# Hybrid decoder step: the S5 tables dealt between preparation and loop, U loaded earlier, gate tiles dealt anew

## The chip, the cores and the metric

One core of a Trainium2 chip runs the kernel. The engines are TensorE (PE, and PEld for its weight loads), VectorE (DVE), ScalarE (ACT), GpSimd (POOL) and SyncE (SP), which here only issues DMAs. The metric is the device time of one execution in microseconds (us), lower is better, given as the median of the runs.

## The reference

One inference step of a one-layer decoder over 1024 prompt positions and 8 x 4 sample positions, in float32. After an RMSNorm one projection gives q, k, v, the S5 input u and two gates:

```python
proj = rmsnorm(x, norm1_g) @ w_in
u = proj[..., U_START:GA_START]          # 512 wide
gate_a = proj[..., GA_START:GS_START]    # 1024 wide
gate_s = proj[..., GS_START:]            # 1024 wide
...                                      # branch A: dilated attention, 12 heads of 64, three groups
acc_re, acc_im, s_re, s_im = lax.associative_scan(
    _complex_scan_combine, (a_re, a_im, bu_re, bu_im), axis=1)   # branch B: S5, 32 groups, 64 complex states
y = C h + D u; y = gelu(y); y = y * sigmoid(y @ w_glu + b_glu)
mix = sigmoid(gate_a) * (attn_out @ w_branch_attn) + sigmoid(gate_s) * (ssm_out @ w_branch_ssm)
x = x + mix @ w_out
...                                      # channel mixer: gated MLP with a width-3 convolution, residual
```

## The kernel before, in words

**Layout.** Activations lie with features on the 128 partitions and positions in the free dimension: T = 1056 columns (1024 prompt and 32 sample positions), as four residues of 264. A product with a weight tile of 128 output features is `product`: its 512 KB of weights are loaded by SP (L153), rounded to a high part by ACT (L154), the low part is made by DVE (L155), then eight steps (`gemm_k`, one for each 128 input features) of nine matmuls of 352 columns each run into three PSUM banks (L173), and an evacuation empties the banks. `fill(n)` places n of these steps into PE's stream.

**Order.** In this part of the kernel PE's order is written out by hand. The order on the other engines and in the DMA queues comes from a scheduler that simulates the program and, among what is ready, goes by the order of the program text. Each engine and each queue then works its list strictly in order. A tile pool hands out a fixed number of buffers for a name; a new use waits until the last readers of the old one are done.

**Preparation of S5** (about 92 to 199 us in the profile). The sixteen gate tiles (eight for gate_s, eight for gate_a) are evacuated by ACT (L464) and stored to `sgd` (L465). PREP + LOOP = 9 of them are spread over the preparation and the S5 loop, 5 lie in the attention loop, the last two (HELD) behind it. Meanwhile:
- `eb` and `gb`, the input and output matrices of the state space, are made by DVE and by POOL. POOL clears both (L645, L646). ACT copies `ctr` into the first slice of gb (L649). POOL makes the other slices from products of `APW` and `ctr` (`bmul`, L624 to L628).
- The rotation tables: for each of 16 pairs of groups (pass i), `TB` x `TB` and `TB` x `TS` (L680) are multiplied and added (L684) into a table of 2 x 256 values a partition. Even i are made by POOL, odd i by DVE; POOL's DMA queue stores all of them to `rtd` in DRAM (L685).
- `Mm`, the matrix of the terms inside a chunk: PE multiplies eb by gb (L692) in four parts, between which `fill(2)` stands; DVE copies each part out of PSUM (L698) and adds D (L701). Two PSUM buffers serve the four parts.
- Then the memory of the preparation is closed and `U`, the S5 input with 32 x 4 rows on the partitions, is read back from DRAM `ud` by 16 DMAs on SP (L711). `ud` was written by the products for u (`u_part`, L313).

**The S5 loop** (about 199 to 300 us), 18 turns over 16 passes. `states(i)`: SP loads table i into `rt` (three buffers, L728); PE multiplies `em` (a transposed eb) by U (L733); DVE rotates the states by the table (L740 to L742), scans twice (L744, L745) and rotates back: n[0] on DVE, n[1] on POOL (L750), then H (L752 to L755). `y_of(i - 2)`: PE multiplies Mm by U and gb by H (L761 to L763), ACT applies gelu. The remaining gate steps are dealt over the turns by `fill`.

**The attention loop** (about 335 to 640 us), 50 turns over 48 blocks in six units. Before unit n its q, k and v products must be done. `due(n)` says how many steps `fill` places into turn n: the steps of all units and of the five gates in `rest` evenly, 160 over 50 turns.

Of the kernel before, what the change touches and what calls it, by code (L numbers as in the profile page):

```python
# [9 lines left out]
F32 = mybir.dt.float32  # L10
# [3 lines left out]
OP = mybir.AluOpType  # L14
# [4 lines left out]
P = 128  # L19
D = 1024  # L20
NB = 8
S4 = 4
C = 264
# [3 lines left out]
KD = D // P  # L27
# [5 lines left out]
AHEAD = 3  # L33
XCH = 264
PREP = 5
LOOP = 4
HELD = 2
NEG = -1e30
EPS = 1e-6
# [59 lines left out]
def body(tc, I, O):  # L99
    nc = tc.nc  # L100
# [3 lines left out]
    def pool(name, bufs, space=None, stack=root, side=None):  # L104
        kw = {} if space is None else {"space": space}
        if space != DRAM:
            kw["reuse_waits"] = "tile"
        if side:
            kw["side"] = side
        return stack.enter_context(tc.tile_pool(name=name, bufs=bufs, **kw))  # L110

    with root:
# [114 lines left out]
        def pending():  # L227
            return len(jobs) * KD + state["left"]
# [224 lines left out]

        s1.close()
        spb = pool("s5m", 1, stack=s2, side="right")


        def gate(which, m):
# [187 lines left out]
            G_.memset(gb[x], 0.0)  # L646
        for x in range(2):
            for g in range(2):
                A_.copy(gb[x][64 * g:64 * g + 64, :, 0, g], ctr[x][64 * g:64 * g + 64])  # L649
        bb = [bp.tile([P, NS, 16], F32, name=f"bb{x}") for x in range(2)]  # L650

        def si_(t):
# [18 lines left out]
        fill(KD * PREP - 8)  # L671
        G_.memset(Mm, 0.0)

        rtp = pool("rtp", 1, stack=bstk)
        rtd = dr.tile([NS, P, 512], F32, name="rtd")
        for i in range(NS):
            E = V_ if i % 2 else G_
            vs = [rtp.tile([P, 2, 256], F32, name=f"v{x}{i % 2}") for x in range(2)]
            for x, lo in enumerate((TB, TS)):
                E.tensor_tensor(vs[x].rearrange("p x (a b) -> p x a b", a=16),  # L680
                                 TB[:, x, None, 16:32, i, None].to_broadcast([P, 2, 16, 16]),
                                 lo[:, :, None, 0:16, i].to_broadcast([P, 2, 16, 16]), OP.mult)
            r_ = rtp.tile([P, 2, 256], F32, name="r", bufs=2)
            E.tensor_tensor(r_, vs[0], vs[1], OP.add)  # L684
            nc.gpsimd.dma_start(rtd[i], r_.rearrange("p x c -> p (x c)"))  # L685
        for i4 in range(4):
            pt = pa.tile([P, 512], F32, name="pa")
# [13 lines left out]
            V_.scalar_tensor_tensor(Mm[:, i], ident, dcol[:, i:i + 1], Mm[:, i], OP.mult, OP.add)  # L701
        bstk.close()
        spr.close()
        spu = pool("s5u", 1, stack=s2, side="right")
        sp1 = pool("s5a", 1, stack=s2)
        sp2 = pool("s5b", 2, stack=s2)
        pa = pool("pa", 8 - PG5, PSUM, stack=s2)
        U = spu.tile([P, NS, C], F32, name="U")
        for m in range(4):
            for s in range(S4):  # L710
                nc.sync.dma_start(U[32 * s:32 * s + 32, 4 * m:4 * m + 4], udv[s][:, 4 * m:4 * m + 4])  # L711

        finb = sp1.tile([P, 2, NS], F32, name="fin")
        fin = [finb[:, x] for x in range(2)]
# [4 lines left out]
        def em_of(i):  # L719
# [3 lines left out]
            ems[i] = sp2.tile([P, 2, P], F32, name="em")  # L723
            A_.copy(ems[i], pt[:, 0:256].rearrange("p (x m) -> p x m", x=2))

        def states(i):
            rt = sp2.tile([P, 2, 256], F32, name="rt", bufs=3)
            nc.sync.dma_start(rt.rearrange("p x c -> p (x c)"), rtd[i])  # L728
            em = ems.pop(i)
            ps = []  # L730
            for x in range(2):
                pS = pa.tile([P, 512], F32, name="pa")
                PE.matmul(pS[:, :C], em[:, x], U[:, i], start=True, stop=True)  # L733
                ps.append(pS)
            for x in range(2):
                A_.copy(SS[x][:, i % 4, i // 4], ps[x][:, 256:264])

            m = [sp2.tile([P, 2, 256], F32, name=f"mm{x}") for x in range(2)]
            for x in range(2):
                V_.tensor_tensor(m[x], ps[x][:, None, :256].to_broadcast([P, 2, 256]), rt, OP.mult)  # L740
            V_.tensor_tensor(m[0][:, 0], m[0][:, 0], m[1][:, 1], OP.add)
            V_.tensor_tensor(m[1][:, 0], m[1][:, 0], m[0][:, 1], OP.subtract)  # L742
            rbc = rho[:, i:i + 1].to_broadcast([P, 256])
            V_.tensor_tensor_scan(m[0][:, 1], rbc, m[0][:, 0], 0.0, OP.mult, OP.add)  # L744
            V_.tensor_tensor_scan(m[1][:, 1], rbc, m[1][:, 0], 0.0, OP.mult, OP.add)  # L745
            Hb = sp2.tile([P, 2, 1 + C], F32, name="H", bufs=3)
            H = [Hb[:, x] for x in range(2)]
            nn_ = [sp1.tile([P, 2, 256], F32, name=f"n{x}") for x in range(2)]
            for x, E in ((0, V_), (1, G_)):
                E.tensor_tensor(nn_[x], m[x][:, 1, None].to_broadcast([P, 2, 256]), rt, OP.mult)  # L750
            G_.memset(Hb[:, :, 0:1], 0.0)
            V_.tensor_tensor(H[0][:, 1:257], nn_[0][:, 0], nn_[1][:, 1], OP.subtract)  # L752
            V_.tensor_tensor(H[1][:, 1:257], nn_[0][:, 1], nn_[1][:, 0], OP.add)
            V_.tensor_copy(finb[:, :, i], Hb[:, :, 256])
            V_.tensor_copy(Hb[:, :, 256:264], h0b[:, :, i])  # L755
            Hs[i] = H

        def y_of(i):
# [6 lines left out]
            if i % 4 == 3:  # L765
                for s in range(S4):
                    nc.sync.dma_start(ydv[s][:, i - 3:i + 1], U[32 * s:32 * s + 32, i - 3:i + 1])

        em_of(0)
        fill(1)  # L770
        base = pending()
# [319 lines left out]

        def due(n):

            return max(0, pending() - base * max(0, NB8 - n) // (NB8 + 2))

        for n in range(NB8 + 2):
            u, blk = divmod(n, 8)
# [429 lines left out]
```

## Time and profile before

| | before |
|---|---|
| median of 3 runs | 1721.08 us (1717.3 to 1724.82) |
| profiled execution | 1719.37 us, its span 1717.5 us |
| PE busy | 1620.5 us, 94% of the span |
| DVE busy | 803.4 us, 47% |
| ACT busy | 492.5 us, 29% |
| POOL busy | 407.3 us, 24% |

The profile is of one execution. Busy time is the time in which an engine works on an instruction; waits, branches and the issuing of DMAs don't count. A row of the timeline is one instruction, or several alike that are merged (x and their number), with its start, its time, its source line, what it writes and reads, and in brackets how long the engine stood idle before it and what released it. PEclk is the share of its full clock that PE was granted.

### The profile page before, as it was taken

The numbers are of one execution on the slowest core, as the hardware profiler recorded it, in microseconds if no ns is written. First come the engines' busy times: TensorE is split into PE (matmuls) and PEld (weight loads), VectorE is DVE, ScalarE is ACT, GpSimd is POOL, SyncE is SP. The second block draws the span as 40 slices with busy tenths as digits, with TensorE's granted clock in tenths as the row PEclk, the third lists the DMA queues.
The fourth block names the chain that finished last, engine by engine and source line by source line (L and its number), as shares of the span: only waits on it lengthen the run. The fifth ranks groups of instructions, "written<-read, shape, count | busy, mean of one in ns | idle before, by whom it ended". The sixth has DMA issues, their size and how long they took to land.

```text
span 1717.5 us, 25878 instructions
## 1 busy us (share of the span) xinstructions
PE 1620.5 (94%) x10431; PEld 1546.7 (90%) x10431; DVE 803.4 (47%) x1461; ACT 492.5 (29%) x945; POOL 407.3 (24%) x463
## 2 busy tenths in 40 slices
PE   5989579999999999898999999999999999999997
PEld 5888478988989889777999999999999999999996
DVE  6668698234433433324724444434344353444455
ACT  5211122234343332415522222121221212111126
POOL 0668323021121322321422121020110101110114
PEclk9999799999999999999999999999999999999999
DMA  8233433354336434686511110211202011020222
GB/s 225 66 118 125 132 99 97 94 142 132 96 84 163 139 106 119 249 272 191 164 50 42 45 50 19 68 34 41 62 24 75 23 53 54 24 64 28 60 61 102
DMA packets 226802, 162.81 MB, mean 95 GB/s; under 512 B 31429, under 2 KB 211119, under 8 KB 226682
## 3 DMA queue, kind: packets, MB, share of 16 engines
q1 hardware_dynamic: 212362, 137.15, 27.4%
q0 software_dynamic: 3968, 13.63, 2.3%
q10 hardware_dynamic: 10352, 10.38, 1.9%
q8 instruction: 82, 1.34, 0.3%
q14 instruction: 38, 0.31, 0.1%
HBM read 131.07 MB, written 32.01 MB: 95 GB/s over the span
## 4 chain that ended last, share of the span: by engine, by line
PE 54%; DMA 3%; ACT 1%; DVE 1%; issue 0%; POOL 0%; DVEq 0%; ACTq 0%; SPq 0%; POOLq 0%
PE pg L173 52%; DMA msd<-go 1%; PE pg L1471 1%; DMA go<-sgd 1%; DMA ck<-sgd 1%; PE pg L143 0%; PE pa L143 0%; DMA cache<-in_cache_kv_w_dram 0%; ACT xl L1279 0%; PE pD L1207 0%; PE pe L143 0%; DVE ml L185 0%; ACT ck L1307 0%; DMA go<-in_x_sample_dram 0%; DVE go L1258 0%
## 5 line engine op out<-in xcount | busy, mean ns | idle before, releaser
L173 PE MATMUL pg<-xh,wlo 128*128 128x352 f32 x1872 | 485.0, 333 | 13.0 <-ACT go L464 9.6
L173 PE MATMUL pg<-xh,whi 128*128 128x352 f32 x1872 | 470.1, 324 | 0.0
L173 PE MATMUL pg<-xl,whi 128*128 128x352 f32 x1872 | 469.0, 324 | 0.0
L173 PEld LDWEIGHTS pg<-xh,wlo 128*128 128x128 f32 x1872 | 331.3, 190 | 24.1 <-ACT go L464 10.4
L173 PEld LDWEIGHTS pg<-xl,whi 128*128 128x128 f32 x1872 | 332.4, 190 | 0.2
L173 PEld LDWEIGHTS pg<-xh,whi 128*128 128x128 f32 x1872 | 332.1, 189 | 0.0
L154 ACT CAST whi<-wraw 128x1024 fp32r<-128x1024 f32 (+2 forms) x154 | 130.9, 850 | 573.5 <-PE pg L173 385.8
L155 DVE TENSOR_TENSOR wlo<-wraw,whi 128x1024 fp32r<-128x1024 f32 (+2 forms) x154 | 159.6, 1036 | 66.8 <-ACT whi L154 64.1
L173 PE MATMUL pg<-hh,wlo 128*128 128x352 f32 x480 | 148.0, 325 | 0.0
L173 PE MATMUL pg<-hl,whi 128*128 128x352 f32 x480 | 147.0, 322 | 0.0
L173 PE MATMUL pg<-hh,whi 128*128 128x352 f32 x480 | 146.5, 323 | 0.0
L1374 POOL COPY ext<-ext 128x510 f32<-128x510 f32 x22 | 15.7, 713 | 522.1 <-DVE ext L1373 522.1
L1401 DVE TENSOR_TENSOR y<-pg,y 128x352 f32<-128x352 f32 x168 | 84.5, 524 | 98.8 <-PE pg L173 98.1
L946 POOL TENSOR_TENSOR qb<-kt,qb 128x512 f32<-128x512 f32 x48 | 63.4, 1334 | 264.4 <-DMA qb<-qd 146.7
L1373 DVE TENSOR_TENSOR ext<-pg,rb 128x352 f32<-128x352 f32 x66 | 32.7, 524 | 154.2 <-PE pg L173 154.2
L173 PEld LDWEIGHTS pg<-hh,wlo 128*128 128x128 f32 x480 | 88.9, 188 | 0.5
L173 PEld LDWEIGHTS pg<-hl,whi 128*128 128x128 f32 x480 | 89.1, 188 | 0.0
L173 PEld LDWEIGHTS pg<-hh,whi 128*128 128x128 f32 x480 | 88.7, 188 | 0.0
L1388 DVE TENSOR_TENSOR go<-pg,cv 128x352 f32<-128x352 f32 x66 | 31.2, 521 | 111.6 <-PE pg L173 111.6
L1382 POOL TENSOR_TENSOR cv<-cv,rb 128x1056 f32<-128x1056 f32 x22 | 54.2, 2464 | 55.0 <-ACT cv L1381 52.6
L991 ACT COPY pTs<-pT 128x256 f32<-128x256 f32 (+1 forms) x48 | 22.6, 471 | 135.0 <-PE pT L143 128.8
L173 PE MATMUL pg<-yh,wlo 128*128 128x352 f32 x144 | 48.0, 344 | 7.0 <-ACT go L464 4.0
(645 smaller groups left out, 2325.0 us busy)
## 6 DMA issues: line engine op xcount, KB each, us to landing
wraw<-in_w_up_dram SPq DMA_DIRECT2D x44, 512.0 KB
wraw<-in_w_in_dram SPq DMA_DIRECT2D x38, 512.0 KB
qb<-qd SPq DMA_DIRECT2D x48, 256.0 KB
wraw<-in_w_down_dram SPq DMA_DIRECT2D x48, 192.0 KB
sgd<-go SPq DMA_DIRECT2D x16, 528.0 KB
kt<-in_cache_kv_w_dram SPq DMA_DIRECT2D x32, 256.0 KB
cache<-in_cache_kv_w_dram POOLq DMA_DIRECT2D x16, 512.0 KB, 6.8
go<-sgd SPq DMA_DIRECT2D x8, 528.0 KB
```

The source lines that it names most:

```text
L154: A_.copy(hi, raw)
L155: E2.tensor_tensor(lo, raw, hi.bitcast(F32), OP.subtract)
L173: PE.matmul(ps[c][:, :CH], wt[:, k0 + k, m0:m0 + P], xt[:, c * CH:(c + 1) * CH], start=k == 0 and j == 0, stop=k == n - 1 and j == 2)
L946: G_.tensor_tensor(qb, kv_, qb, OP.mult)
L991: A_.copy(pTs[:, :2 * n * P], pT[:, :2 * n * P])
L1373: V_.tensor_tensor(ef[:, 2 * C + c * CH:2 * C + (c + 1) * CH], ps[c][:, :CH], rb2[:, cs(c)], OP.mult)
L1374: G_.tensor_copy(e[:, 0:2, 1:256], e[:, 4:6, 0:255])
L1382: G_.tensor_tensor(cv, cv, rb2, OP.mult)
L1388: V_.tensor_tensor(t[:, cs(c)], ps[c][:, :CH], cv[:, cs(c)], OP.mult)
L1401: V_.tensor_tensor(y[m][:, cs(c)], ps[c][:, :CH], y[m][:, cs(c)], OP.add)
L1471: PE.matmul(pt, sx[:, j, k] if b == 8 else hs_[k][j][:, cols(b)], w[:, 0, hq], start=k == 0 and w is wlo, stop=k == len(ws) - 1 and w is w ...
```

## The change

Five edits, all in or around S5.
- `LOOP` goes from 4 to 6: eleven gate tiles are spread over the preparation and the S5 loop, and three are left for the attention loop.
- The tables. All are made by POOL. The first EARLY = 8 are made in the preparation, with one buffer for each intermediate, and are stored to `rtd` as before. The other eight are made in the loop, straight into `rt`, without DRAM; `table(i + 1)` is called in `states(i)`. `tc.issue_after(early.ins)` places them behind the last early table in POOL's queue.
- U is allocated, and its 16 DMAs are written, ahead of the gate products.
- The four copies of ctr into gb go from ACT to POOL.
- `due` deals three steps to a turn until the products of the units are used up, and the steps of the three gates over the last ten turns.

```diff
-LOOP = 4
+LOOP = 6
+EARLY = 8
...
         spb = pool("s5m", 1, stack=s2, side="right")
+        spu = pool("s5u", 1, stack=s2, side="right")
+        U = spu.tile([P, NS, C], F32, name="U")
+        for m in range(4):
+            for s in range(S4):
+                nc.sync.dma_start(U[32 * s:32 * s + 32, 4 * m:4 * m + 4], udv[s][:, 4 * m:4 * m + 4])
...
-                A_.copy(gb[x][64 * g:64 * g + 64, :, 0, g], ctr[x][64 * g:64 * g + 64])
+                G_.tensor_copy(gb[x][64 * g:64 * g + 64, :, 0, g], ctr[x][64 * g:64 * g + 64])
...
-        rtp = pool("rtp", 1, stack=bstk)
-        rtd = dr.tile([NS, P, 512], F32, name="rtd")
-        for i in range(NS):
-            E = V_ if i % 2 else G_
-            vs = [rtp.tile([P, 2, 256], F32, name=f"v{x}{i % 2}") for x in range(2)]
+        def rotation(o, i, vs):
             for x, lo in enumerate((TB, TS)):
-                E.tensor_tensor(vs[x].rearrange("p x (a b) -> p x a b", a=16),
+                G_.tensor_tensor(vs[x].rearrange("p x (a b) -> p x a b", a=16),
                                  TB[:, x, None, 16:32, i, None].to_broadcast([P, 2, 16, 16]),
                                  lo[:, :, None, 0:16, i].to_broadcast([P, 2, 16, 16]), OP.mult)
-            r_ = rtp.tile([P, 2, 256], F32, name="r", bufs=2)
-            E.tensor_tensor(r_, vs[0], vs[1], OP.add)
+            return G_.tensor_tensor(o, vs[0], vs[1], OP.add)
+
+        rtp = pool("rtp", 1, stack=bstk)
+        rtd = dr.tile([EARLY, P, 512], F32, name="rtd")
+        for i in range(EARLY):
+            vs = [rtp.tile([P, 2, 256], F32, name=f"v{x}") for x in range(2)]
+            r_ = rtp.tile([P, 2, 256], F32, name="r")
+            early = rotation(r_, i, vs)
             nc.gpsimd.dma_start(rtd[i], r_.rearrange("p x c -> p (x c)"))
...
+        rts = {}
+
+        def table(i):
+            rts[i] = rt = sp2.tile([P, 2, 256], F32, name="rt", bufs=3)
+            if i < EARLY:
+                nc.sync.dma_start(rt.rearrange("p x c -> p (x c)"), rtd[i])
+            else:
+                with tc.issue_after(early.ins):
+                    rotation(rt, i, [sp1.tile([P, 2, 256], F32, name=f"v{x}") for x in range(2)])
+
         def states(i):
-            rt = sp2.tile([P, 2, 256], F32, name="rt", bufs=3)
-            nc.sync.dma_start(rt.rearrange("p x c -> p (x c)"), rtd[i])
+            rt = rts.pop(i)
+            if i + 1 < NS:
+                table(i + 1)
...
+        table(0)
         em_of(0)
...
-            return max(0, pending() - base * max(0, NB8 - n) // (NB8 + 2))
+            last = NB8 - 8
+            done = min(3 * (n + 2), 15 * KD) if n < last else 15 * KD + KD * len(rest) * (n + 1 - last) // 10
+            return max(0, pending() - (base - done))
```

## Rows read from the trace of the kernel before

**Rows 1.** Windows: start:end length, busy us PE, PEld, DVE, ACT, POOL (x), PEclk, DMA
```profile
92.00:198.82 106.82, 78.96 (x668) 75.99 (x667) 79.95 (x76) 14.90 (x29) 75.44 (x55) 0.89 0.35 116
198.82:300.50 101.68, 86.52 (x452) 77.75 (x453) 86.33 (x189) 27.09 (x80) 27.07 (x30) 0.93 0.39 109
...
335.50:640.00 304.50, 299.32 (x2033) 270.71 (x2033) 117.22 (x364) 119.81 (x327) 67.22 (x54) 0.99 0.46 123
```
**Rows 2.** PE's waits from 92 to 300 us: total, times, longest
```profile
PE pa L762 <- DVE H L755: 14.9, 3, 9.0
PE pa L143 <- DVE Mm L698: 10.5, 1, 10.5
PE pg L173 <- ACT go L464: 6.8, 1, 6.8
PE pa L733 <- DMA U<-ud: 6.4, 1, 6.4
PE pa L692 <- DVE Mm L698: 4.1, 2, 3.8
```
**Rows 3.** Windows right behind PE's waits of 6.8, 6.4 and 1.6 us
```profile
110.60:113.40 2.80, 2.78 (x9) 2.79 (x10) 1.02 (x1) 1.72 (x3) 2.80 (x3) 0.50 0.47 186
...
198.80:202.50 3.70, 3.67 (x11) 3.29 (x12) 0.00 (x0) 0.33 (x2) 0.00 (x0) 0.50 1.12 218
...
295.60:298.00 2.40, 2.40 (x13) 2.21 (x14) 0.00 (x0) 1.12 (x3) 0.53 (x1) 1.00 0.06 16
```
**Rows 4.** Timeline of PE: a gate step, the first Mm matmul, two passes' starts
```profile
119.38 0.65 PE L173 MATMUL pg<-xh,wlo 128*128 128x352 f32 x3
...
120.84 0.65 PE L173 MATMUL pg<-xh,wlo 128*128 128x352 f32 x3
...
152.94 1.93 PE L692 MATMUL pa<-gb,eb 128*32 128x128 f32 x64
...
223.78 1.05 PE L733 MATMUL pa<-U,em 128*128 128x264 f32 x4
...
227.66 1.05 PE L733 MATMUL pa<-U,em 128*128 128x264 f32 x4
```
**Rows 5.** Timeline of SP's queue: the issuing of U's loads
```profile
194.34 7.45 SPq L711 DMA_DIRECT2D U<-ud  x16
```
**Rows 6.** Timeline of POOL: a copy, gb, parts of tables, an n
```profile
76.59 0.40 POOL L583 COPY TS<-TB 128x256 f32<-128x256 f32 x1 [0.38 <-DVE TB L490]
...
106.99 2.24 POOL L646 MEMSET gb<- 128x2560 f32 x1 [11.54 <-issue]
...
138.39 5.27 POOL L628 TENSOR_TENSOR gb<-g,g 64x1024 f32<-64x1024 f32 x2
...
157.66 1.37 POOL L680 TENSOR_TENSOR v<-TB 128x512 f32<-128x512 f32 x1
158.98 1.37 POOL L680 TENSOR_TENSOR v<-TB,TS 128x512 f32<-128x512 f32 x1
...
179.45 1.26 POOL L684 TENSOR_TENSOR r<-v,v 128x512 f32<-128x512 f32 x1
...
228.15 1.60 POOL L750 TENSOR_TENSOR n<-mm,rt 128x512 f32<-128x512 f32 x1 [1.60 <-issue]
```
**Rows 7.** Timeline of DVE: two multiplies of a table, loop instructions
```profile
156.26 1.06 DVE L680 TENSOR_TENSOR v<-TB 128x512 f32<-128x512 f32 x1
157.23 4.04 DVE L680 TENSOR_TENSOR v<-TB,TS 128x512 f32<-128x512 f32 x1
...
228.51 0.69 DVE L740 TENSOR_TENSOR mm<-pa,rt 128x512 f32<-128x512 f32 x1
...
231.85 0.17 DVE L755 COPY H<-h 128x16 f32<-128x16 f32 x1
```
**Rows 8.** Window of 27.9 us inside the S5 loop, columns as in rows 1
```profile
223.70:251.60 27.90, 27.90 (x156) 25.59 (x155) 24.85 (x57) 8.65 (x29) 7.22 (x10) 1.00 0.36 106
```
**Rows 9.** DVE's weight subtraction in that window: count, busy us, mean ns
```profile
L155 DVE TENSOR_TENSOR wlo<-wraw,whi 128x1024 fp32r<-128x1024 f32 x1 | 1.2, 1220 | 0.0
```

More of the change, by code (lines that the diff above doesn't have):

```diff
@@ L703, in body @@
         spr.close()
-        spu = pool("s5u", 1, stack=s2, side="right")
         sp1 = pool("s5a", 1, stack=s2)
@@ L707, in body @@
         pa = pool("pa", 8 - PG5, PSUM, stack=s2)
[L708 to L711, printed above, removed]
         finb = sp1.tile([P, 2, NS], F32, name="fin")
```

## The prediction

> **What bounds the kernel now.** I read the page's busy times first: PE is busy for 94% of the span, no other engine for half of it, so a gain must come from PE's idle time or from its clock. The windows by stage show where those lie: from 92 to 300 us PE is busy for 165.5 of 208.5 us at a granted clock of 0.89 and 0.93, in the attention loop for 299.3 of 304.5 at 0.99 [rows 1]. The change works in the first stretch, so I sum PE's waits there [rows 2]: in the preparation 27.8 us (6.8 for ACT's evacuation of a gate, 4.1 and 10.5 for DVE's copies of Mm, 6.4 for U), in the S5 loop 14.9 (DVE's H, three times). Behind each wait of 3.8 us or more PE works for some 3 us at about half clock; behind one of 1.6 us it doesn't [rows 3]. Time lost is busy time x (1 - clock): 1.4 behind the 6.8, 1.5 and 1.6 behind the two long Mm waits, 1.9 behind U: 6.4. In the loop there are two such stretches, 1.5 + 1.4 = 2.9. PE's work itself is fixed: a step of a gate is nine matmuls in 1.46 us, and a loop pass takes 3.88 us with one step in it, so 2.42 without [rows 4].
>
> Upper end of the gain: 27.8 + 6.4 + 14.9 + 2.9 = **52.0 us**.
>
> **The change part by part.**
>
> *U early.* The 16 issues hold SP for 7.45 us [rows 5] and now come before the gates' stores and weight loads. Each waits for its ud store, and a weight load behind it waits too. PE doesn't see it as long as weights are one product ahead (8 x 1.46 = 11.7 us): cost 0, at most 7.5 once. The wait of 6.4 and its 1.9 go, and rt's first loads no longer stand behind U.
>
> *gb copies to POOL.* ACT's copies stood in its queue until POOL had cleared gb at 109.2 [rows 6], and the gate's evacuation stood behind them. They leave, so the 6.8 goes, with its 1.4 of clock. POOL gains four copies, each between 0.40 (a copy of as many elements a partition, on twice the partitions) and 1.37 (a multiply of twice as many): 1.6 to 5.5, taken 1.6, since the copy is the same operation. Behind them on POOL wait the products that make gb, then the tables.
>
> *Eight tables early, on POOL.* DVE loses all its tables. A multiply of one cost it 1.06 when POOL stood still and 4.04 when it met two multiplies of POOL, 1.37 each [rows 6, 7]: the DVE instruction is held for as long as POOL's. Without them the Mm copies follow their matmuls; the waits of 4.1 and 10.5 go, with 3.1 of clock. What is late next? The gb products. POOL ended them at 143.7 [rows 6], with two of its own tables between them and DVE's in the way; PE, rid of 6.8 + 1.4, comes to its first Mm matmul at 152.9 - 8.2 = 144.7 [rows 4]. With 1.6 of copies gb comes at 145.3 if the order stays, near 140 if products and tables run unstretched. I take **+1**. A table on POOL is 1.37 + 1.37 + 1.26 = 4.0, so the six still to come after gb end near 170, when the loop begins: that starts at 198.8 - 27.8 - 4.5 = 166.5, and the 1.9 of clock that was lost behind U goes as well. Its first H can be late by 0 to 9.0 us (the longest wait for H); behind the last early tables I take **+3**. The loop's last pass had a wait of 1.6 for H; I keep **+2** for it.
>
> *Eight tables in the loop, two more gates.* PE has 43 steps left for 18 turns instead of 27: 2.39 x 1.46 + 2.42 = 5.92 us a pass. DVE's pass is shorter: 24.85 us hold five passes, the L740 pair of a sixth (1.4) and one weight subtraction (1.2) [rows 8, 9], so 4.5; six subtractions over 16 passes add 0.45: 5.0. Without tables DVE would stop setting the pace, and the loop's 14.9 + 2.9 would go.
>
> But the tables of passes 8 to 15 need a buffer of rt, of which there are three, so table i + 3 starts only when pass i has read its own: eight passes carry one each, and n of the next pass stands behind it on POOL. There POOL has n (a multiply of the same size, 1.37) and a table: 5.4 us. L740, which reads PSUM, kept its 0.69 beside POOL's n [rows 6, 7]; what reads SBUF alone doesn't. So DVE's 5.0 - 1.2 = 3.8 (L740 overlaps its neighbours by a little) and POOL's 5.4 go one after the other: 9.2 us a pass against PE's 5.92. PE has some slack: two turns (11.8) lie between a pass's first matmul and the use of its H, which came 231.85 + 0.17 - 223.78 = 8.2 us after it; 3.6 us. Stall: 8 x 3.28 - 3.6 = **+23**. Bounds: 12 if n always falls beside L740, as in the row (7.8 a pass); 0 if all is hidden; 32 if L740 is held too (10.4 a pass). I take 23 because the held multiply (4.04) is the nearest row. Clock lost in these waits falls into time in which PE waits anyway.
>
> *due.* Two gates (16 steps, 23.4 us) leave the attention loop for the S5 loop; PE's sum is unchanged. Attention gets 3 steps a block, in the last ten 2.4. PE's idle time in it was 5.2 us [rows 1]. Thinner filling can add 0 to as much again; I take **+2**. Were attention not bound by PE, this would cost up to 23.4: its 98% busy excludes that.
>
> Sum: 52.0 gained; 1 + 3 + 2 + 23 + 2 = 31 given back; **-21.0**. The profiled execution took 1719.37 us (span 1717.5), so 1698.4; it stands 1.7 below the median of 1721.08, so I predict **1700**.
>
> **Rivals.**
> (a) *The tables hide.* POOL uses the moments in which DVE waits or reads PSUM, and the loop runs at PE's pace. For it: POOL is busy for only 27 of the loop's 102 us [rows 1]. Against: DVE is busy for 86 of them. Then 23 is 0: **1677**.
> (b) *gb comes behind tables.* If the scheduler's order on POOL puts more early tables ahead of the gb products, PE stands at the first Mm matmul. Each costs 4.0 beyond a slack of some 4: four give 12, six 20: **1712 to 1720**. For it: two were already between them. Against: the others came after gb.
> (c) *POOL and DVE in a strict chain, slower than before.* Place: passes 5 to 13. n of a pass stands on POOL behind a table, and H waits for n. If DVE gets nothing else done meanwhile, a pass is POOL's 5.4, four hand-overs of one DVE instruction (0.69 each, 2.8) and DVE's 5.0: 13.2. Stall 8 x 7.28 - 3.6 = 55: **1732**. It decides from 11.9 us a pass upward, where 8 x (p - 5.92) - 3.6 + 8 reaches 52.0. Against: DVE's order mixes two passes, so it has other work while it waits for n.
> (d) *POOL's multiplies are slower in the loop.* At twice DVE's 1.06 a table is 2.12 + 2.12 + 1.26 = 5.5, a pass 10.7, the stall 35: **1712**. Against: 1.37 in the rows, 1.3 times. The Trainium skill has this factor: "GPSIMD Engine Reference", section 4.1 (Engine selection), puts two-input elementwise work on GpSimd at about twice VectorE's time and would leave it on VectorE; the rows bear out the direction, not the size.
>
> **How the numbers follow.** A measurement of this kernel tells about 0.5% from no change: faster is below 1712.5, slower above 1729.7. The forecast, 1689 to 1709 with its bounds of 12 and 32, has 0.50; (a) 0.20; (b) 0.12; (c) 0.14; (d) 0.04. Faster: 0.50 + 0.20 + 0.04 of (b) + 0.02 of (d) = 0.76. Same: 0.08 of (b), 0.02 of (d), 0.06 of (c) = 0.16. Slower: 0.08, the rest of (c). The range goes from 1675, which takes in (a), to 1720, which takes in (b) and (d); above it lies (c), below it a loop without any new wait.
>
> **What would show it.** No wait of PE for ACT near 104 and none for Mm or U; the loop's first matmul near 167; passes of about 6 us up to pass 5, then of 9 us with DVE instructions of 1.5 to 4 us beside POOL's tables, and PE waiting for H some 3 us in each; the S5 loop's end still near 300, but two gates further on; the attention loop some 21 us shorter, with no more than 7 us of waits. Wrong if passes with tables run near 6 us (then 1677), if the first Mm matmul waits for POOL, if passes take 12 us or more, or if SP's U loads hold a gate's weights.

## The result, and the profile after

The changed kernel took **1700.92 us**, the median of four runs (1697.35 to 1703.09), against 1721.18 for the kernel before: a ratio of 0.9881, 95% interval 0.9853 to 0.9908. That is faster by more than the 0.5% that can be told from no change, 0.9 us from the predicted 1700 and inside the range. The profiled execution took 1697.35 us with a span of 1695.4; the forecast for the profiled one was 1698.4.

The sum came out, but its two largest terms did not: the preparation gave less than predicted and the tables in the loop cost less. The lines below show both. Line numbers have moved: L143 of before is L144, L173 is L174, L698 is L707 (copies of Mm), L701 is L710 (additions of D to Mm), L733 is L748 (S), L740 is L755, L755 is L770, L762 is L777.

Four starts of TensorE's work and the end of the span, in us:

| | before | after | moved by |
|---|---|---|---|
| first matmul of the loop | 198.8 | 175.7 | -23.1 |
| first logits of the attention | 334.5 | 337.1 | +2.6 |
| last logits of the attention | 640.0 | 616.7 | -23.3 |
| first matmul into `pD`, the output of the sample attention | 709.6 | 689.4 | -20.2 |
| end | 1717.5 | 1695.4 | -22.1 |

The windows of the kernel after (columns as in [rows 1]) are the preparation, the loop up to its first table and from there to its end, the attention, and the stretch behind it:

```profile
92.00:175.70 83.70, 77.22 (x681) 75.26 (x680) 45.58 (x50) 13.74 (x26) 69.08 (x49) 0.97 0.48 144
175.70:215.30 39.60, 39.60 (x226) 37.41 (x226) 35.45 (x70) 12.36 (x35) 12.40 (x17) 0.99 0.35 108
215.30:297.40 82.10, 67.14 (x340) 60.19 (x339) 74.50 (x119) 16.28 (x48) 48.67 (x41) 0.92 0.17 53
...
337.00:616.70 279.70, 275.82 (x1889) 245.30 (x1890) 114.53 (x361) 115.84 (x321) 68.09 (x54) 1.00 0.47 125
616.70:689.40 72.70, 64.90 (x422) 61.02 (x418) 26.16 (x56) 23.49 (x43) 18.11 (x17) 0.93 0.51 173
```

In the loop's first 40 us TensorE has no wait at all. What is left lies at two places: 6.5 us in the preparation, and 15.2 us in the passes with a table and the turns behind them. PE's waits of the kernel after from 85 to 320 us (total, times, longest) name them:

```profile
PE pa L748 <- DVE mm L755: 8.7, 3, 5.9
PE pa L144 <- DVE Mm L707: 6.5, 1, 6.5
PE pa L777 <- DVE H L770: 3.5, 3, 2.5
PE pa L144 <- DVE mm L755: 3.0, 1, 3.0
```

Against [rows 2], the waits for ACT's evacuation (6.8), for U (6.4) and for H (14.9) are gone or small, and one for Mm is still there. What follows three of the waits (6.5, 5.9 and 2.4 us; the last window begins 1.3 us before its wait ends), columns as in [rows 1]:

```profile
172.50:176.00 3.50, 3.43 (x12) 3.46 (x13) 3.50 (x3) 0.37 (x1) 3.50 (x4) 0.50 0.00 0
236.70:242.20 5.50, 5.47 (x18) 4.94 (x19) 4.27 (x9) 0.54 (x2) 2.63 (x3) 0.55 0.00 1
...
217.00:220.00 3.00, 1.68 (x10) 1.61 (x11) 2.93 (x6) 0.17 (x1) 0.64 (x1) 1.00 0.00 0
```

As in [rows 3], the granted clock is near half behind the long waits and full behind the short one. Busy time x (1 - clock) over all such stretches is 1.7 us behind the Mm wait and 5.8 in the loop.

**Why the Mm copies are still late.** DVE in the preparation of the kernel after, four additions of D (L710), a weight subtraction (L156) and the third group of copies:

```profile
150.28 5.25 DVE L710 SCALAR_TENSOR_TENSOR Mm<-ident,SM,Mm 128x128 f32<-128x128 f32 x4
...
160.69 4.09 DVE L156 TENSOR_TENSOR wlo<-wraw,whi 128x1024 fp32r<-128x1024 f32 x1
164.82 1.99 DVE L707 COPY Mm<-pa 32x512 f32<-32x512 f32 x4
```

and POOL beside them, in the early tables:

```profile
161.00 1.38 POOL L683 TENSOR_TENSOR v<-TB 128x512 f32<-128x512 f32 x1
162.33 1.36 POOL L683 TENSOR_TENSOR v<-TB,TS 128x512 f32<-128x512 f32 x1
163.77 2.16 POOL L686 TENSOR_TENSOR r<-v,v 128x512 f32<-128x512 f32 x1
...
171.99 1.26 POOL L686 TENSOR_TENSOR r<-v,v 128x512 f32<-128x512 f32 x1 [2.51 <-DMA rtd<-r]
```

The subtraction starts just ahead of a POOL multiply and ends behind the second one (4.09 us; [rows 9] have 1.22); POOL's addition is stretched in turn (2.16 for 1.26). Each addition of D in the group shown takes 1.3 us, in the later ones 0.8 to 1.0; free ones take 0.28, as run 8 shows. The copies of Mm read PSUM and keep their time (1.99 us for four, here and in run 8), but they stand in DVE's queue behind these.

How much this costs PE depends on how the instructions of the two engines fall against one another. The wait for Mm in run 6 and in run 12 below, whose early tables and Mm are as in the kernel after:

```profile
PE pa L144 <- DVE Mm L707: 3.7, 1, 3.7
...
PE pa L144 <- DVE Mm L707: 7.3, 1, 7.3
```

It is 3.5 to 4.0 us in runs 1, 4, 5, 6, 9 and 10, where the first two groups of additions take 2.4 to 3.0 us, and 6.5 and 7.3 in the kernel after and in run 12, where they take 3.2 to 5.3. In those six the loop's first matmul comes at 171.1 to 172.9, not at 175.7. So some 3 us of the 6.5 come from how they fell in this trace.

**What a pass with a table is made of.** One pass of the kernel after, POOL first, then DVE:

```profile
247.68 1.63 POOL L765 TENSOR_TENSOR n<-mm,rt 128x512 f32<-128x512 f32 x1 [2.08 <-DVE mm L760]
249.38 1.53 POOL L686 TENSOR_TENSOR rt<-v,v 128x512 f32<-128x512 f32 x1
250.99 1.43 POOL L683 TENSOR_TENSOR v<-TB 128x512 f32<-128x512 f32 x1
252.38 1.39 POOL L683 TENSOR_TENSOR v<-TB,TS 128x512 f32<-128x512 f32 x1
255.86 1.65 POOL L765 TENSOR_TENSOR n<-mm,rt 128x512 f32<-128x512 f32 x1 [2.08 <-DVE mm L760]
```

```profile
247.51 0.67 DVE L765 TENSOR_TENSOR n<-mm,rt 128x512 f32<-128x512 f32 x1
249.34 0.43 DVE L767 TENSOR_TENSOR H<-n,n 128x256 f32<-128x256 f32 x1 [1.16 <-POOL H L766]
249.68 1.52 DVE L768 TENSOR_TENSOR H<-n,n 128x256 f32<-128x256 f32 x1
251.12 0.68 DVE L755 TENSOR_TENSOR mm<-pa,rt 128x512 f32<-128x512 f32 x1
251.73 0.72 DVE L769 COPY fin<-H 128x2 f32<-128x2 f32 x1
252.36 0.68 DVE L755 TENSOR_TENSOR mm<-pa,rt 128x512 f32<-128x512 f32 x1
252.96 0.85 DVE L770 COPY H<-h 128x16 f32<-128x16 f32 x1
...
255.70 0.67 DVE L765 TENSOR_TENSOR n<-mm,rt 128x512 f32<-128x512 f32 x1
```

DVE waits 1.16 us for POOL's n and is then held three times, each time to within 0.3 us of the end of a POOL instruction: the second H (1.52 for 0.42), and the two small copies (0.72 and 0.85 for 0.16), 2.3 us in all. L755, which reads PSUM, keeps its 0.68 in the middle of POOL's multiplies. The Trainium skill ("SBUF — State Buffer", section "Who interferes with whom") states this rule: a VectorE instruction with two inputs in SBUF contends with a GpSimd one that reads SBUF, one with at most one such input (outside the two-port modes, which plain copies can enter) does not, and the loser stands still for the whole instruction. The trace agrees: H, with two inputs in SBUF, takes 1.52 instead of 0.42 here, and L755, with one in PSUM, keeps its 0.68. From n to n the pass took 8.2 us; from POOL's n at 211.94 to that at 281.37 eight passes took 8.68 each.

### The profile page after: what moved, and what is told of

Its sections match the earlier page's. It is cut to its first block, busy times and chain, and to the rows that moved or that the text cites. A ratio compares the mean times of both kernels' runs of the same rounds, so it can differ in the third digit from the quotient of the medians.

```text
span 1695.4 us, 25830 instructions
## 1 busy us (share of the span) xinstructions
PE 1623.4 (96%) x10431; PEld 1547.1 (91%) x10431; DVE 791.0 (47%) x1437; ACT 490.8 (29%) x941; POOL 434.9 (26%) x483
## 3 DMA queue, kind: packets, MB, share of 16 engines
q8 instruction: 82, 1.34, 0.3%
## 4 chain that ended last, share of the span: by engine, by line
PE 55%; DMA 2%; ACT 1%; DVE 1%; POOL 1%; issue 1%; DVEq 0%; ACTq 0%; POOLq 0%; SPq 0%
PE pg L174 53%; DMA msd<-go 1%; PE pa L144 1%; DMA ck<-sgd 1%; DMA go<-sgd 0%; DMA cache<-in_cache_kv_w_dram 0%; PE pD L1225 0%; PE pg L1489 0%; ACT go L1493 0%; PE pg L144 0%; DVE hh L1506 0%; PE pe L144 0%; DVE ml L186 0%; ACT xl L1297 0%; PE pD L1228 0%
## 5 line engine op out<-in xcount | busy, mean ns | idle before, releaser
L174 PE MATMUL pg<-xh,wlo 128*128 128x352 f32 x1872 | 484.2, 332 | 3.0 <-ACT pt__5401 L870 1.5
L174 PE MATMUL pg<-xh,whi 128*128 128x352 f32 x1872 | 470.5, 325 | 0.0
L174 PE MATMUL pg<-xl,whi 128*128 128x352 f32 x1872 | 468.5, 324 | 0.0
L174 PEld LDWEIGHTS pg<-xh,wlo 128*128 128x128 f32 x1872 | 329.5, 189 | 14.5 <-issue 5.6
L174 PEld LDWEIGHTS pg<-xh,whi 128*128 128x128 f32 x1872 | 332.2, 189 | 0.0
L174 PEld LDWEIGHTS pg<-xl,whi 128*128 128x128 f32 x1872 | 331.7, 189 | 0.3
L156 DVE TENSOR_TENSOR wlo<-wraw,whi 128x1024 fp32r<-128x1024 f32 (+2 forms) x154 | 162.2, 1053 | 99.5 <-ACT whi L155 96.7
L174 PE MATMUL pg<-hh,wlo 128*128 128x352 f32 x480 | 148.0, 325 | 0.0
L174 PE MATMUL pg<-hl,whi 128*128 128x352 f32 x480 | 147.0, 322 | 0.0
L174 PE MATMUL pg<-hh,whi 128*128 128x352 f32 x480 | 146.5, 323 | 0.0
L174 PEld LDWEIGHTS pg<-hh,wlo 128*128 128x128 f32 x480 | 88.9, 188 | 0.5
L174 PEld LDWEIGHTS pg<-hl,whi 128*128 128x128 f32 x480 | 89.1, 188 | 0.0
L174 PEld LDWEIGHTS pg<-hh,whi 128*128 128x128 f32 x480 | 88.7, 188 | 0.0
L174 PE MATMUL pg<-yh,wlo 128*128 128x352 f32 x144 | 48.2, 345 | 4.1 <-ACT go L471 3.4
```

The costliest lines, as they stand in the source:

```text
L156: E2.tensor_tensor(lo, raw, hi.bitcast(F32), OP.subtract)
L174: PE.matmul(ps[c][:, :CH], wt[:, k0 + k, m0:m0 + P], xt[:, c * CH:(c + 1) * CH], start=k == 0 and j == 0, stop=k == n - 1 and j == 2)
```

## The experiments

Each ratio is to the kernel before, timed on the same chip; the kernel after stands at 0.9881. Differences to the kernel after in us are between medians from different chips, on which the kernel before had medians of 1719.2 to 1722.6, so 2 to 3 us of such a difference can be the chip. Places in time come from one trace a kernel, and the stretch behind the first matmul into `pD`, 1006.0 us in the kernel after, took up to 1011.9 in kernels that change nothing there (runs 2 and 3).

**1. The loop without its tables.**

```diff
-            if i < EARLY:
-                nc.sync.dma_start(rt.rearrange("p x c -> p (x c)"), rtd[i])
-            else:
-                with tc.issue_after(early.ins):
-                    rotation(rt, i, [sp1.tile([P, 2, 256], F32, name=f"v{x}") for x in range(2)])
+            nc.sync.dma_start(rt.rearrange("p x c -> p (x c)"), rtd[i % EARLY])
```

> The changed kernel, but POOL makes no tables in the loop: passes 8 to 15 load the first eight tables a second time, so eight of the sixteen tables are left out of the computation. Theory (the lock): in the changed kernel passes with a table take 8.7 us, because POOL's table and DVE's instructions that read SBUF alone go one after the other; PE loses 14.2 us in waits in those passes and 5.8 us at half clock. Without the tables the passes run at PE's pace of about 6 us, these waits are gone and the time falls by about 17 to 20 us, to 1681 to 1684 us. Rival 1 (the tables hide; the waits come from DVE's own work and its order): no change, 1699 to 1702 us, and the passes stay over 8 us. Rival 2 (half each): 1690 us.

1677.85 us, ratio 0.9748 (0.9730 to 0.9767): 23.1 us below the kernel after. PE's waits from 85 to 320 us in this kernel, all but one of 0.7 us:

```profile
PE pa L144 <- DVE Mm L707: 3.9, 1, 3.9
PE pa L773 <- DVE H L766: 1.0, 1, 1.0
PE pa L744 <- DVE mm L751: 0.7, 2, 0.4
```

The loop's waits are all but gone, and its clock loss with them (granted clock 1.00). From the loop's first matmul to the first logits this kernel takes 20.2 us less (141.2 against 161.4), close to the 15.2 of waits and 5.8 of clock read above: that is what the eight tables cost. The rest of the 23.1 isn't theirs: the loop begins 4.5 us sooner (171.2), and so it does in runs 4, 5 and 6, which make the tables (171.1 to 171.5). Rival (a)'s time of 1677 is that of a loop in which the tables cost nothing.

**2. The copies of Mm on ACT.**

```diff
-                V_.tensor_copy(Mm[32 * s:32 * s + 32, i4 * 4:i4 * 4 + 4, 32 * s:], pv[32 * s:32 * s + 32, :, 32 * s:])
+                A_.copy(Mm[32 * s:32 * s + 32, i4 * 4:i4 * 4 + 4, 32 * s:], pv[32 * s:32 * s + 32, :, 32 * s:])
```

> The changed kernel, but the sixteen copies of Mm out of PSUM are done by ACT instead of DVE. In the changed kernel PE still waits 6.5 us for the last Mm copy: the copies stand in DVE's queue behind additions of D and a weight subtraction that POOL's early tables hold up (four additions take 3.2 to 5.3 us instead of 1.1). Theory: with the copies out of that queue PE's wait goes, with 1.7 us of half clock; the loop's first matmul comes at 167 to 168 instead of 175.7, and the time falls by 5 to 8 us, to 1693 to 1696 us. Rival: the start of the loop is set by POOL's last early table (its end at 176 us) and by DVE's additions anyway; then PE only waits later, for the first passes, and the time stays at 1699 to 1702 us.

1701.40 us, ratio 0.9883 (0.9865 to 0.9902): no gain. The Mm wait is gone and the loop's first matmul comes at 167.5 instead of 175.7, where the prediction had put it (near 167). But DVE in this kernel shows what holds its first loop instruction:

```profile
173.80 1.46 DVE L803 TENSOR_TENSOR fx<-h,APW 128x128 f32<-128x128 f32 x1 [7.39 <-POOL r L686]
175.18 1.27 DVE L755 TENSOR_TENSOR mm<-pa,rt 128x512 f32<-128x512 f32 x2
```

An instruction from behind the loop (fx), placed early in DVE's queue, waits 7.39 us for POOL's last early table. PE then waits three times between 175 and 194 us, 5.9 us together.

**3. The copies into gb back on ACT.**

```diff
-                G_.tensor_copy(gb[x][64 * g:64 * g + 64, :, 0, g], ctr[x][64 * g:64 * g + 64])
+                A_.copy(gb[x][64 * g:64 * g + 64, :, 0, g], ctr[x][64 * g:64 * g + 64])
```

> The changed kernel with one part undone: the four copies into gb are back on ACT. Theory of the prediction: ACT's evacuation of the first gate waits behind them until POOL has cleared gb, PE waits 6.8 us near 104 and runs 1.4 us longer at half clock, so 7 to 8 us more: 1708 to 1709 us. Rival: PE's lost time is absorbed, because the end of the preparation is set by DVE and POOL (PE waits 6.5 us for Mm at its end); then that wait shrinks by as much and the time stays within 2 us of 1701.

1707.32 us, ratio 0.9926 (0.9907 to 0.9946): 6.4 us above the kernel after. PE's waits have one for ACT again:

```profile
PE pg L174 <- ACT go L471: 3.7, 1, 3.7
PE pa L144 <- DVE Mm L707: 3.7, 1, 3.7
```

The wait for ACT is 3.7, not 6.8: POOL has cleared gb 1.2 us sooner (108.0 against 109.2), and PE comes to this wait 1.8 us later (at 105.6 instead of 103.8). The Mm wait is 2.8 shorter than in the kernel after, as in most of the runs. By the time, the move is worth 6.4 us of the 8.2 that the prediction had counted for it. The traces don't place all of it: the loop begins 2.8 us later than in the kernel after, though 7.2 later than in run 4, and 5.7 us lie behind the first matmul into `pD`.

**4. U loaded where it was.**

```diff
-        spu = pool("s5u", 1, stack=s2, side="right")
-        U = spu.tile([P, NS, C], F32, name="U")
-        for m in range(4):
-            for s in range(S4):
-                nc.sync.dma_start(U[32 * s:32 * s + 32, 4 * m:4 * m + 4], udv[s][:, 4 * m:4 * m + 4])
...
         spr.close()
+        spu = pool("s5u", 1, stack=s2, side="right")
+        U = spu.tile([P, NS, C], F32, name="U")
+        for m in range(4):
+            for s in range(S4):
+                nc.sync.dma_start(U[32 * s:32 * s + 32, 4 * m:4 * m + 4], udv[s][:, 4 * m:4 * m + 4])
```

> The changed kernel with one part undone: U is allocated and its sixteen loads are written behind the preparation again, as before. Theory of the prediction: the place in the program text decides; U comes late again, PE waits 6 us for it at the start of the loop and runs 2 us longer at half clock: 1707 to 1709 us. Rival: U was late because its memory lay where the tables' buffers were, which the smaller buffers of the changed kernel have ended; then the scheduler issues the loads early all the same, and the time stays at 1699 to 1703 us. The issue time of U's loads on SP's queue (104 in the changed kernel, 194 before) tells them apart.

1702.39 us, ratio 0.9892 (0.9877 to 0.9907): the same. SP's queue in the kernel after and in this one:

```profile
104.00 7.52 SPq L461 DMA_DIRECT2D U<-ud  x16
```

```profile
104.78 7.54 SPq L712 DMA_DIRECT2D U<-ud  x16
```

Both issue U at 104 to 105, 90 us before the kernel before did [rows 5]. Where the loads stand in the text makes no difference. In the kernel before SP's queue waited at this line for the stores of the tables:

```profile
SPq L711 <- DMA rtd<-r: 18.9, 2, 9.5
```

Neither of the two others has such a wait. That U took the place of the tables' buffers, which the change has made smaller, fits this; it is argued from the code, not tried by itself.

**5. Two gates fewer in the loop, with the old `due`.**

```diff
-LOOP = 6
+LOOP = 4
...
-            last = NB8 - 8
-            done = min(3 * (n + 2), 15 * KD) if n < last else 15 * KD + KD * len(rest) * (n + 1 - last) // 10
-            return max(0, pending() - (base - done))
+            return max(0, pending() - base * max(0, NB8 - n) // (NB8 + 2))
```

> The deal of the gate tiles is undone alone: four whole gates in the loop and the old division in the attention, everything else as in the changed kernel. Theory A (the two added gates fill waits that the tables leave on TensorE in the loop): in the kernel without loop tables a pass lasts about 5.9 us with these gates, in the changed kernel 6.0 without and 8.7 with a table on POOL; with two gates fewer TensorE has about 1.3 us a pass less to do, the passes with a table stay at 8.7, and those without fall from 6.0 to about 4.7, so the loop shrinks by only some 10 us where 23.4 us of gates go back into the attention: 1710 to 1716. Theory B (where the gates run makes no difference, TensorE being the bound at either place): 1701. Theory C (the attention had room for these gates beside its own waits, and the loop is better off without them): below 1698.

1712.34 us, ratio 0.9958 (0.9942 to 0.9974): 11.4 us above the kernel after. From the loop's first matmul to the first logits it is 5.1 us shorter, though 23.4 us of work have left it. PE's longest sum of waits in the loop, and the loop's window:

```profile
PE pa L777 <- DVE H L770: 23.1, 9, 7.6
```

```profile
171.50:288.70 117.20, 90.11 (x421) 79.25 (x421) 113.33 (x188) 24.34 (x75) 69.43 (x61) 0.87 0.19 55
```

DVE is busy (held time included) for 113 of 117 us: DVE, held by POOL's tables, sets this loop's length, and the gates fill what would be waits.

**6. Two gates more in the loop.**

```diff
-LOOP = 6
+LOOP = 8
```

> Two gates more in the loop (eight instead of six), nothing else changed. Theory A (the lock's waits in the loop can be filled further): the eight passes with a table last 8.7 us and TensorE has 5.9 us of work in each; 1.3 us more a pass closes half of the gap, so some 8 x 1.3 = 10 us of the added 23.4 are free, and the clock loss of 5.8 us falls with the waits: 1688 to 1695. Theory B (the gates are dealt evenly over all passes, and the attention, with 23.4 us fewer to fill its own waits, gives the gain back): 1699 to 1704.

1699.65 us, ratio 0.9889 (0.9870 to 0.9907): the same. The loop behaves as theory A has it, 14.8 us longer for 23.4 us of work; but from the first logits to the first matmul into `pD` it is only 16.7 us shorter. There PE waits, with less to fill it:

```profile
PE pa L144 <- DVE R L1202: 5.4, 1, 5.4
PE pT L144 <- ACT pTs L1007: 5.4, 2, 5.1
```

That is not all of it: the loop begins 4.6 us sooner than in the kernel after (171.1), and behind the first matmul into `pD` this kernel takes 8.8 us more (1014.8 against 1006.0), 4.1 of them in a longer wait for DVE's `go` (L1276, 4.8 against 0.7). Why that stretch is so long was not tried; so theory B is not shown to be the whole reason.

**7. Mm on ACT, and fx with memory of its own.**

In addition to run 2's edit:

```diff
-                fo = sp2.tile([P, NS, NB], F32, name="fx", bufs=1)
+                fo = sp1.tile([P, NS, NB], F32, name="fx")
```

> The copies of the Mm blocks on ACT, as in the run before, and in addition the fx buffer taken from the pool of single buffers, so that the operation on VectorE that was held by the early tables' memory has other memory. Theory A (that held operation is what kept the gain of the ACT copies back): VectorE's first L755 comes some 7 us sooner, TensorE keeps the 7 us that it had won at the loop's start: 1693 to 1697. Theory B (the first table of the loop and n on POOL stand behind the early tables, which last until 173 us in any order, so the loop's second pass waits for POOL instead): 1700 to 1703.

1701.28 us, ratio 0.9894 (0.9877 to 0.9911): again no gain. DVE now begins the loop at 168.15, 7 us sooner than in run 2, and meets POOL's last early table and the first multiplies of the loop's tables there:

```profile
168.15 1.29 DVE L755 TENSOR_TENSOR mm<-pa,rt 128x512 f32<-128x512 f32 x2 [1.71 <-issue]
169.47 3.04 DVE L756 TENSOR_TENSOR mm<-mm,mm 128x256 f32<-128x256 f32 x1
...
173.95 1.76 DVE L759 TENSOR_TENSOR_SCAN mm<-SM,mm 128x256 f32<-128x256 f32 x1
```

L756 takes 3.04 us instead of 0.42 and the scan 1.76 instead of 0.69. The first n on POOL comes at 177.56, against 180.46 in the kernel after: of 8.4 us won at the loop's first matmul 2.9 are left, and PE waits 1.7 and 3.5 us in the next passes. POOL makes two multiplies of the loop's first table (at 173.60 and 175.13) between the last early table and that n.

**8. Four early tables instead of eight.**

```diff
-EARLY = 8
+EARLY = 4
...
-            if i < EARLY:
-                nc.sync.dma_start(rt.rearrange("p x c -> p (x c)"), rtd[i])
+            if i < 8:
+                nc.sync.dma_start(rt.rearrange("p x c -> p (x c)"), rtd[i % EARLY])
```

> Four early tables instead of eight; passes 4 to 7 load the first four again (four tables are left out, the eight of the loop are made as in the changed kernel). POOL is then done with the early tables some 16 to 20 us sooner, at about 155 us. Theory A (what TensorE still waits for the Mm copies ahead of the loop is VectorE held by the early tables: its additions of D took 3.2 to 5.3 us for four, where four free ones take 1.1): from 157 us on the additions take 1.1 us for four, the wait for the Mm copies falls from 6.5 to below 2 us and the loop's first matmul comes at 167 to 170 us instead of 175.7; of that, as in the run with Mm on ACT, the loop's first passes give nothing back because n on POOL no longer stands behind early tables: 1693 to 1697 in all. Theory B (VectorE's and TensorE's order alone makes the wait, each transposition and copy following the other): wait and first matmul as before, 1699 to 1702. Theory C (the loop's later passes, bound by the tables, swallow what is won ahead of them): first matmul at 167 to 170 us, the time still 1699 to 1702.

1693.90 us, ratio 0.9832 (0.9814 to 0.9849): 7.0 us below the kernel after. DVE's additions of D, the first group beside the end of POOL's last early table and the first multiplies of the loop's tables, the second when POOL has stopped:

```profile
150.63 4.42 DVE L710 SCALAR_TENSOR_TENSOR Mm<-ident,SM,Mm 128x128 f32<-128x128 f32 x4
...
157.28 1.14 DVE L710 SCALAR_TENSOR_TENSOR Mm<-ident,SM,Mm 128x128 f32<-128x128 f32 x4
```

The Mm wait is gone with DVE still making the copies, the loop's first matmul comes at 167.9, and the loop gives nothing back: the first n is at 172.26, PE's first wait ends at 210.0, and the loop is 1.0 us shorter to the first logits (160.4 against 161.4). Together with runs 2 and 7 this settles the cause: what the preparation still lost was the time for which POOL's tables held DVE, and taking Mm from DVE only moves that time into the loop's first pass. The size is less sure. The two traces differ by 3.3 us at the end (1692.1 against 1695.4), since this one takes 4.0 us more from the first logits to the first matmul into `pD` and 1.5 more behind it, and against runs 4, 5 and 6 the loop begins 3 us sooner, not 7.7.

**9. The loop's tables on DVE.**

```diff
-        def rotation(o, i, vs):
+        def rotation(o, i, vs, E=G_):
...
-                with tc.issue_after(early.ins):
-                    rotation(rt, i, [sp1.tile([P, 2, 256], F32, name=f"v{x}") for x in range(2)])
+                rotation(rt, i, [sp1.tile([P, 2, 256], F32, name=f"v{x}") for x in range(2)], V_)
```

> The eight tables of the loop are made by VectorE instead of POOL, nothing else changed. Theory A (what costs is the time that POOL holds VectorE out, 1.4 + 1.4 + 1.3 us of POOL's operations a table): VectorE's own two multiplications and addition take 1.06 + 1.06 + 0.7 = 2.8 us, a pass goes from 8.7 to about 7.8 and the eight to some 7 us less: 1692 to 1697. Theory B (VectorE is then the only bound of these passes and the table stands in its queue ahead of the copies that TensorE waits for): 9 us a pass or more, 1703 to 1710.

1693.53 us, ratio 0.9851 (0.9829 to 0.9873): 7.4 us below the kernel after by the medians, some 5 by the ratios, whose intervals overlap, so the profile has to tell. From the loop's first matmul to the first logits it takes 7.0 us less (154.4 against 161.4). DVE makes a table in 2.8 us of its own (the addition and the second multiply are shown), and these are not held:

```profile
230.31 0.69 DVE L686 TENSOR_TENSOR rt<-v,v 128x512 f32<-128x512 f32 x1
...
232.58 1.01 DVE L683 TENSOR_TENSOR v<-TB,TS 128x512 f32<-128x512 f32 x1
```

Seven passes, from POOL's n at 219.25 to that at 272.08, take 7.55 us each instead of 8.68. What is left of the hold lies at n: DVE's took 1.38 us once (0.67 free), and POOL's 3.5 twice (1.3 to 1.7 in the other passes).

**10. The same, with the gates' matmuls dealt three to two.**

```diff
+        share = [3 if EARLY <= i + 1 < NS else 2 for i in range(NS + 2)]
+        left = lambda i: base * sum(share[i + 1:]) // sum(share)
...
-            fill(pending() - base * (NS + 1 - i) // (NS + 2) - 1)
+            fill(pending() - left(i) - 1)
...
-            fill(pending() - base * (NS + 1 - i) // (NS + 2))
+            fill(pending() - left(i))
```

> The loop's tables on VectorE, as in the run before, and the gates' matmuls that fill the loop are dealt three to two in favour of the eight passes that make a table, instead of evenly. Theory A (what is left of the loop's stall is that these passes last about 7.5 us by VectorE and TensorE has 5.9 us of work in them, while the others last 5.9 us by TensorE): about half a step, 1 us, more in each of the eight closes more than half of the 11 us of waits and 3.5 us of clock that are left there: 1685 to 1690. Theory B (the other passes then fall to VectorE's own time of 5.3 us plus the order of its queue, and the waits only move): 1691 to 1695.

1688.47 us, ratio 0.9818 (0.9789 to 0.9847), 5.1 below the run before it; the intervals overlap, so the profile has to tell. The loop's windows of run 9 and of this one:

```profile
172.90:288.50 115.60, 104.03 (x565) 96.08 (x565) 108.06 (x212) 28.55 (x83) 34.11 (x37) 0.96 0.24 75
```

```profile
172.80:284.60 111.80, 103.41 (x565) 93.18 (x564) 103.19 (x207) 28.94 (x83) 32.18 (x36) 0.99 0.25 80
```

The same matmuls are done in 3.8 us less: PE's idle time falls from 11.6 to 8.4 and the clock rises from 0.96 to 0.99, as its waits are short now (1.8 at most).

**11. The same, with run 7's two edits: the best version.**

> The run before (tables of the loop on VectorE, matmuls dealt three to two) with the Mm copies on ACT and fx in the pool of single buffers. Theory A (the loop's start is held by the early tables on POOL, and once the later passes are not, the 3.5 us that TensorE waits for the Mm copies are won): 3 us below the run before, 1682 to 1687. Theory B (as with POOL's tables, the won time is waited out in the loop's first passes, for n on POOL behind the early tables): the same as the run before.

1685.13 us, ratio 0.9796 (0.9770 to 0.9822), 15.8 us below the kernel after. The preparation's window has PE busy throughout,

```profile
92.00:167.70 75.70, 75.70 (x681) 73.98 (x680) 38.61 (x37) 20.42 (x42) 63.25 (x43) 1.00 0.53 156
```

and of the 5.1 us by which the loop begins sooner than in run 10 all are still there at the first logits (319.9 against 325.3). The median is 3.3 us lower, which by the intervals alone is not certain. Why the won time stays here and not in run 7 was not tried by itself; the traces show one difference. With the loop's tables on DVE, POOL's first n comes at 174.94 with no multiply between it and the last early table, where in run 7 the two multiplies of the loop's first table put it at 177.56, and DVE's first scan takes 0.69 instead of 1.76.

**12. The old `due` alone.**

> Only the new division of the gate tiles over the attention is undone (the even one of before is back), with six gates still in the loop. Theory A (the new division costs nothing or a little, as the prediction put it: up to 2 us): 1699 to 1701. Theory B (the new division is worth something: the attention came out 4.5 us shorter than the two gates taken from it explain, 25.9 instead of 21.4 us): 1703 to 1707.

1700.51 us, ratio 0.9881 (0.9854 to 0.9908): the same. The attention is 3.5 us longer than in the kernel after (283.2 against 279.7) and the stretch behind it 3.5 shorter (69.2 against 72.7). The new division moves steps from one to the other and is worth nothing.

## Why the prediction was right, and where its steps were wrong

*U early*: the wait and its clock went, but the step's reason ("loads written earlier") was wrong; run 4 shows that the place in the text does nothing. PE waited for no weight load, as was taken.

*gb copies to POOL*: right. The wait of 6.8 went, and undoing the move costs 6.4 us of time, though only part of it can be placed. A pair of copies took 0.85 on POOL, so four take 1.7 (predicted 1.6); gb was done at 139.5, ahead of PE's first Mm matmul at 146.1, so the +1 was 0.

*Eight tables early*: here the step failed. "Without them the Mm copies follow their matmuls" took only DVE's own tables from DVE's queue; that POOL's tables, which [rows 6, 7] show holding a DVE multiply, would hold the additions of D between the copies was not carried through. 6.5 us of wait and 1.7 of clock stayed, and the loop began at 175.7 instead of near 167 (1.6 of the difference lies ahead of the first gate). Runs 2, 7 and 8 show the cause: without that hold it begins at 167.3 to 167.9, and four early tables fewer are worth 7.0 us by the medians. The size is not fixed: with the same early tables six other kernels wait 3.5 to 4.0 us and begin the loop at 171.1 to 172.9. The +3 for the first H behind the last early tables was the same cost seen at another place: not there in the kernel after, 5.9 and 5.3 us in runs 2 and 7.

*Eight tables in the loop*: the mechanism was right, the size too large. Predicted were 9.2 us a pass, 23 us of stall, and 2 for the last wait beside the 3; measured were 8.68 and 21.0 (20.2 by run 1). A pass was put together as all of POOL's 5.4 behind DVE's 3.8; POOL's n and table together took 6.0 in the pass shown (n alone 1.63, near the 1.60 of [rows 6], not the 1.37 of a multiply), so the size came from taking the two wholly "one after the other". In the trace DVE is held for 2.3 us of a table's 4.0 to 4.4, because L755 falls beside its multiplies, and waits 1.2 for n: 4.5 + 1.2 + 2.3 = 8.0 of the 8.2 shown. On the other side "clock lost in these waits falls into time in which PE waits anyway" was wrong: 15.2 us are waits and 5.8 are clock, which falls behind a wait, where PE has work again. PE's wait also showed at another line: mostly at S (L748), whose bank L755 frees late because it stands behind the held H in DVE's queue, and only 3.5 us at H.

*due*: -21.4 predicted for the attention; it came out 25.9 shorter, the stretch behind it 3.1 longer, together -22.8. The +2 was 0, and run 12 shows that the division has no part in it.

So the sum: up to the loop 8.2 us worse than predicted (-23.1 against -27.8 - 4.5 + 1 = -31.3), in the loop 6.0 better (from its first matmul to the first logits +25.7 against 23.4 of gates + 28 of stalls - 19.7 of waits and clock = +31.7), in the attention and behind it 1.4 and 1.9 better. The total of -22.1 against -21.0 agrees because two errors of opposite sign, both about the same hold, nearly cancel: that the forecast came so close is luck.

*The rivals*: (a) needed the hold to be absent, and run 1 gives its time once the tables are left out. (b) did not come: gb's products stood ahead of all but two early tables. (c) did not: DVE mixed two passes, as argued. (d) did not: a multiply on POOL took 1.34 to 1.52 in the loop. Its opposite had not been thought of: to move the tables to DVE, though slower in sum of busy time there, is faster by some 5 to 7 us.

## What to carry to other kernels

Work that is given to POOL beside a busy DVE can cost DVE up to the time of POOL's instructions, not nothing (here 2.3 us of a table's 4.0 to 4.4); price it instruction by instruction, with those that read PSUM left out, and compare it with what DVE would need to do the work itself (here 2.8 us of its own against 3.5 of holding and waiting). Carry such a hold to everything that stands in DVE's queue beside it, small additions and copies too, and to the instructions that wait behind those; how large it is changes with how the two queues fall against one another, so one trace is not its size. Where one engine sets a loop's pass, deal the filling matmuls by pass, more to the longer ones, before more of them are taken from a later stage that needs them too.

## What the runs showed of the hardware that was not expected

- The hold doesn't go by the size of the DVE instruction: a copy of 2 elements a partition took 1.2 us (0.16 free), an addition of D 1.3 (0.28), the scan 1.76 (0.69). One DVE instruction can stand through two of POOL's in a row (4.09 us), and then stretches POOL's third (2.16 for 1.26).
- Two waits of about the same length left different clocks: behind 2.40 us the granted clock stayed at 1.00, behind one of 2.54 it was 0.64 over the next 4.8 us, behind one of 2.96 it was 0.71 over 5.8:

```profile
263.70:269.50 5.80, 5.59 (x21) 4.95 (x22) 5.73 (x10) 0.81 (x3) 2.95 (x2) 0.71 0.31 90
274.50:279.30 4.80, 4.78 (x18) 4.10 (x18) 3.63 (x7) 0.56 (x2) 3.20 (x4) 0.64 0.45 113
```

  So the wait of 2.54 cost two thirds more than its length (4.78 x 0.36 = 1.7 us), and the one of 2.40 nothing more. Why they differ is open.
